# The recurrent group of a hybrid decoder layer, with the order of four engines written out by hand

## The chip, the cores and the metric

The kernel runs on one core of one Trainium2 chip. The metric is the device time of one execution in microseconds (us). Before the change it is 588.33 us, the median of three runs (588.04 to 588.38).

## The reference

One decoder layer for 512 tokens of width 1024, all in float32. The part that matters here, shortened:

```python
h = rms_norm(x, g_pre_mix)
q, k, v, xr, gr = split(h @ w_in)                # 512 columns each
attn = moba_attention(q, k, v, rel_bias)         # 8 heads of 64; causal, T5 bias
xr  = causal_dwconv(xr, w_conv_lru) + b_conv_lru # 4 taps along the tokens, per channel
r = sigmoid(blockdiag(xr, w_r) + b_r)            # 8 blocks of 64 channels
i = sigmoid(blockdiag(xr, w_i) + b_i)
log_a = -8 * r * softplus(-lam)
a, u = exp(log_a), sqrt(-expm1(2 * log_a)) * (i * xr)
lru = scan(h_t = a_t * h_(t-1) + u_t) * gelu(gr)
x = x + rms_norm(concat(attn, lru) @ w_out, g_post_mix)
x = x + rms_norm(ffn(rms_norm(x, g_pre_ffn)), g_post_ffn)   # 2816 hidden, conv of 3 taps, GLU
```

## The kernel before, in words

Tokens lie in four tiles of 128 (`NT`), the width in eight (`KD`). Each float32 product is three matmuls of a faster format: an operand is split into an upper part h (a cast on ACT, line 84) and a lower part l (a subtraction on DVE, line 85), and `mm3` (lines 79 to 81) adds hh, hl and lh in one PSUM bank. Weights are split in the same way (`split_w`), after a load of 1 MB on SP's queue into one of two `raw` buffers; the split parts have four buffers, `wh` and `wl`.

The recurrent group runs from the start to line 382. `norm_transpose` squares a token tile on ACT with a row sum, makes the reciprocal root in a few 128x1 steps on ACT and DVE (`rstd_of`), multiplies on DVE (`hn`), transposes on PE against the identity (`ptr`) and splits the result into `hT`. `keep_warm` puts matmuls on ones in between; the weight row `g_pre_mix` is spread over the partitions by four small matmuls (`gpre`, line 207). Small parameters come in rows and are transposed into `par`. `pfb` is the bias of each distance, `fb`, which goes to DRAM as `fbd` and is written out 128 times as `toep` for the attention.

For each of the four channel tiles the x branch is projected (`px`), convolved (line 325 on ACT, 327 three times on DVE), split (`xs`) and multiplied with the two gate matrices (`pg`, in the two "sc" banks); lines 337 to 348 turn that into decay and input, with the scales `kpos` and `kneg`. These come from a softplus of `lam`, a chain of 128x4 instructions on DVE (lines 270 to 287: a series in Horner form). The value projection (`pv`) and the gate branch (`pgr`, then GeLU) are 96 matmuls each. At the end the scan (line 381) and the product go to `mixT`. The attention follows: `head_pair` loads, splits and projects q and k (`pq`).

Nothing in this part has an order written by hand, but for the warm-ups and `gpre` (`keep_in_program_order`). The framework's scheduler lays out each engine's instructions by its own costs. PSUM has eight banks: three "mm", two "sc", two "tr", one "av"; whoever takes a bank waits for the readers of its last contents.

Of the kernel before, what the change touches and what calls it, by code (L numbers as in the profile page):

```python
# [12 lines left out]
F32 = mybir.dt.float32  # L13
# [5 lines left out]
P = 128  # L19
# [33 lines left out]
def hybrid_layer(  # L53
# [51 lines left out]
    nc.sync.dma_start(g_row, g_pre_mix)  # L105
    nc.sync.dma_start(xres[:, 0], x_v[:, 0])
# [27 lines left out]

    def norm_transpose(t, g, hT, pool):

        hn = pool.tile([P, D], F32, tag="hn", name="hn", bufs=4)
        sq = pool.tile([P, D], BF16, tag="sqn", name="sqn")
        ss = cp.tile([P, 1], F32, tag="ss", name="ss", bufs=8)
        nc.scalar.activation(sq, xres[:, t], AF.Square, accum_out=ss)  # L140
        r = rstd_of(ss, consts, "rpre")
        w = D // len(g)
        for n, gn in enumerate(g):
            hs = slice(n * w, (n + 1) * w)
            nc.vector.scalar_tensor_tensor(
                hn[:, hs], xres[:, t, hs], r, gn, op0=ALU.mult, op1=ALU.mult)
# [34 lines left out]
    nc.gpsimd.memset(graw, 0.0)  # L181
    for g, w in enumerate((w_r[0], w_i[0])):
        wv = w.rearrange("(t b) c d -> b c t d", b=2)
        for b in range(2):
            nc.sync.dma_start(graw[64 * b:64 * b + 64, g, :, 64 * b:64 * b + 64], wv[b])
# [6 lines left out]
    warm = pp.tile([P, 512], BF16, name="warm")
    nc.vector.memset(warm, 1.0)
    pwarm = bank("pwarm", "av")

    def keep_warm(n):

        for _ in range(n):
            tc.keep_in_program_order(nc.tensor.matmul(
                pwarm, warm[:, 0:P], warm, start=True, stop=True))  # L200

    keep_warm(3)
    ones = cp.tile([1, P], F32, name="ones")
    nc.vector.memset(ones, 1.0)
    gpre = [bank(f"gpre{n}", "sc") for n in range(2)]
    for n in range(2):
        tc.keep_in_program_order(nc.tensor.matmul(
            gpre[n], ones, g_row[:, n * 512:(n + 1) * 512], start=True, stop=True))
    keep_warm(4)

    for t in range(NT):
        norm_transpose(t, gpre, hT, pp)
        if t < 2:
            keep_warm(3)

    split(gw[0], gw[1], graw)
# [16 lines left out]
    nc.vector.tensor_copy(par, ppar[:, 0:80 + P])  # L233

# [72 lines left out]
    gl = lp.tile([P, NT, S], F32, name="gl")  # L307

    def xr_block(t):
        return split_w(raw_xr[t // 2][:, :, (t % 2) * P:(t % 2 + 1) * P], KD, P), bank("px", "mm")  # L310

    first = [xr_block(t) for t in range(2)]
    for c0, c1 in ((0, S // 2), (S // 2, S)):
        for w, px in first:
            project(w, px, c0, c1)
    for t in range(NT):
        if t < 2:
            px = first[t][1]
        else:
            if t == 2:  # L320
                raw_xr.append(load_raw(w_in[:, XR0 + 256:XR0 + 512], KD, 256))
            w, px = xr_block(t)
            project(w, px)
        c = xc[:, t]
        nc.scalar.activation(c, px, AF.Identity, scale=w_conv_l(3, t), bias=col(16 + t))
        for d in range(1, 4):
            nc.vector.scalar_tensor_tensor(
                c[:, d:], px[:, :S - d], w_conv_l(3 - d, t), c[:, d:], op0=ALU.mult, op1=ALU.add)
        xs = [lp.tile([P, S], F32R, tag=f"xs{i}", name=f"xs{i}") for i in "hl"]
        split(xs[0], xs[1], c)  # L330
        pg = [bank(f"pg{g}", "sc") for g in range(2)]
        for g in range(2):
            mm3(pg[g], at(gw, slice(None), g, t), (xs[0], xs[1]), True, True)


        a, g, y = av[:, t], gv[:, t], gl[:, t]
        nc.vector.tensor_scalar(a, pg[0], col(20 + t), 0.0, op0=ALU.add, op1=ALU.min)
        nc.scalar.activation(g, pg[0], AF.Abs, scale=0.5, bias=half_b[:, t:t + 1])
        nc.scalar.activation(y, pg[1], AF.Tanh, scale=0.5, bias=half_b[:, 4 + t:5 + t])
        nc.vector.scalar_tensor_tensor(c, y, 1.0, c, op0=ALU.add, op1=ALU.mult)  # L340
# [4 lines left out]
        nc.scalar.activation(a, g, AF.Exp, scale=kneg(t))  # L345
        nc.scalar.activation(g, g, AF.Tanh, scale=kpos(t))
# [4 lines left out]
    pv = [bank(f"pv{t}", ("tr", "tr", "av", "mm")[t]) for t in range(NT)]  # L351
    for c in range(2):
        raw = load_raw(w_in[c * 512:(c + 1) * 512, 2 * DA:3 * DA], 4, DA)
        for u in range(2):
            w = split_w(raw[:, 2 * u:2 * u + 2], 2, DA)
            for j in range(2):
                k = 4 * c + 2 * u + j
                for t in range(NT):
                    mm3(pv[t], at(hT, slice(None), k, slice(t * P, (t + 1) * P)),
                        at(w, slice(None), j), k == 0, k == KD - 1)  # L360

    def gr_block(t):
        if t % 2 == 0:
            raw_gr.append(load_raw(w_in[:, GR0 + t * P:GR0 + t * P + 256], KD, 256))
        return split_w(raw_gr[-1][:, :, (t % 2) * P:(t % 2 + 1) * P], KD, P)

    raw_gr = []
    w_gr = [gr_block(t) for t in range(NT)]
    for t in range(NT):
        src = pv[t].rearrange("p (a s d) -> p a s d", s=2, d=DH)  # L370
# [336 lines left out]
```

## Time and profile before

| | before |
|---|---|
| median of three runs | 588.33 us |
| profiled execution | 589.05 us, span 587.3 us |
| PE (TensorE matmul) | 574.3 us busy, 98% of the span |
| DVE / ACT / POOL | 360.1 (61%) / 278.4 (47%) / 2.8 us (0%) |
| DMA moved | 59.62 MB, mean 102 GB/s |

The span is the time that the profile covers. PE's busy time counts pipelined matmuls with a modelled end, so the distance between starts tells its pace better than the busy share. L84 is line 84 of the kernel. `hTh` and `hTl` are the two parts of `hT`. In brackets stands the idle time ahead of an instruction, and what ended it.

### The profile page before, as it was taken

What the parts mean: (1) busy time and instruction counts of PE and PEld (TensorE: products, weight loads), DVE (VectorE), ACT (ScalarE), POOL (GpSimd) and SP (SyncE); (2) the same over time, 40 slices, a digit from 0 to 9 for tenths busy, and PEclk for the clock granted to TensorE, in tenths of its full rate; (3) what the DMA queues carried; (4) which work ended last, traced back from release to release, by engine and by line L of the source; (5) the groups of instructions that cost most, each with busy time, mean ns of one, the idle gap of its engine ahead of it and who ended that gap; (6) DMA issues with size and microseconds to landing.
All of it is one profiled execution on the core that took longest, in us unless ns stands there. A gap on an engine that the chain in (4) does not pass through costs nothing.

```text
span 587.3 us, 7000 instructions
## 1 busy us (share of the span) xinstructions
PE 574.3 (98%) x2717; PEld 472.0 (80%) x2717; DVE 360.1 (61%) x665; ACT 278.4 (47%) x455; POOL 2.8 (0%) x10
## 2 busy tenths in 40 slices
PE   8999999999999999999999999999999999999995
PEld 4877888777788879988888888888888888888884
DVE  5969694798896895656656656656656521241225
ACT  6639953777775762534434443443444322132121
POOL 1000000000000000000000000000000000000000
PEclk9999999999999999999999999999999999999999
DMA  7562436233100624003413413412424223232103
GB/s 235 195 212 72 144 99 186 73 108 108 56 17 25 211 89 144 1 15 129 143 30 114 145 40 104 143 50 95 144 68 137 82 72 105 94 125 71 37 0 143
DMA packets 52265, 59.62 MB, mean 102 GB/s; under 512 B 2448, under 2 KB 41568, under 8 KB 52233
## 3 DMA queue, kind: packets, MB, share of 16 engines
q1 hardware_dynamic: 51201, 57.61, 30.3%
q10 hardware_dynamic: 1032, 1.57, 0.8%
q8 instruction: 21, 0.34, 0.2%
q14 instruction: 11, 0.09, 0.0%
HBM read 57.06 MB, written 3.69 MB: 103 GB/s over the span
## 4 chain that ended last, share of the span: by engine, by line
PE 90%; DVE 4%; ACT 3%; DMA 2%; issue 1%; DVEq 0%
PE pup L80 14%; PE pup L81 14%; PE pup L79 14%; PE py L80 8%; PE py L81 8%; PE py L79 8%; PE pq L79 2%; PE pq L80 2%; PE pq L81 2%; PE pav L471 2%; DMA raw<-in_w_up_dram 2%; PE ptp L461 1%; PE px L81 1%; PE px L79 1%; PE px L80 1%; PE pv L79 1%
## 5 line engine op out<-in xcount | busy, mean ns | idle before, releaser
L85 DVE TENSOR_TENSOR wl<-raw,wh 128x1024 fp32r<-128x1024 f32 x82 | 100.1, 1221 | 124.8 <-ACT wh L84 124.5
L84 ACT CAST wh<-raw 128x1024 fp32r<-128x1024 f32 x82 | 85.6, 1048 | 143.3 <-PE py L81 72.2
L81 PE MATMUL pup<-h2Th,wl 128*128 128x512 f32 x320 | 124.5, 389 | 0.0
L80 PE MATMUL pup<-h2Tl,wh 128*128 128x512 f32 x320 | 124.5, 389 | 0.0
L79 PE MATMUL pup<-h2Th,wh 128*128 128x512 f32 x320 | 124.3, 389 | 0.0
L80 PEld LDWEIGHTS pup<-h2Tl,wh 128*128 128x128 f32 x320 | 60.1, 188 | 12.5
L79 PEld LDWEIGHTS pup<-h2Th,wh 128*128 128x128 f32 x320 | 60.0, 188 | 12.5
L81 PEld LDWEIGHTS pup<-h2Th,wl 128*128 128x128 f32 x320 | 60.1, 188 | 12.3
L79 PE MATMUL py<-wh,acth 128*128 128x512 f32 x176 | 68.9, 391 | 0.0
L81 PE MATMUL py<-wh,actl 128*128 128x512 f32 x176 | 68.8, 391 | 0.0
L80 PE MATMUL py<-wl,acth 128*128 128x512 f32 x176 | 68.8, 391 | 0.0
L79 PEld LDWEIGHTS py<-wh,acth 128*128 128x128 f32 x176 | 33.1, 188 | 7.2
L81 PEld LDWEIGHTS py<-wh,actl 128*128 128x128 f32 x176 | 33.1, 188 | 7.2
L80 PEld LDWEIGHTS py<-wl,acth 128*128 128x128 f32 x176 | 33.1, 188 | 7.2
L629 DVE SCALAR_TENSOR_TENSOR yu<-pup,par,yu 128x511 f32<-128x511 f32 (+1 forms) x44 | 33.0, 749 | 4.3 <-ACT yu L627 3.5
L636 ACT ACTIVATE yg<-yg 128x512 f32<-128x512 f32 x22 | 13.9, 633 | 45.0 <-DVE yg L629 45.0
L629 DVE SCALAR_TENSOR_TENSOR yg<-pup,par,yg 128x511 f32<-128x511 f32 (+1 forms) x44 | 32.8, 746 | 2.0 <-ACT yg L627 1.2
L637 DVE TENSOR_TENSOR yu<-yu,yg 128x512 f32<-128x512 f32 x22 | 15.2, 692 | 18.3 <-ACT yg L636 18.3
L79 PE MATMUL pq<-hTh,wh 128*128 128x512 f32 x64 | 25.4, 397 | 0.0
L81 PE MATMUL py<-wh,mixTl 128*128 128x512 f32 x64 | 25.4, 396 | 0.0
L81 PE MATMUL pq<-hTh,wl 128*128 128x512 f32 x64 | 25.3, 395 | 0.0
L79 PE MATMUL py<-wh,mixTh 128*128 128x512 f32 x64 | 25.2, 394 | 0.0
(199 smaller groups left out, 940.2 us busy)
## 6 DMA issues: line engine op xcount, KB each, us to landing
raw<-in_w_up_dram SPq DMA_DIRECT2D x22, 1024.0 KB, 5.2
raw<-in_w_down_dram SPq DMA_DIRECT2D x10, 1024.0 KB, 5.3
raw<-in_w_in_dram SPq DMA_DIRECT2D x5, 1024.0 KB
rawqk<-in_w_in_dram SPq DMA_DIRECT2D x8, 512.0 KB, 5.3
raw<-in_w_out_dram SPq DMA_DIRECT2D x4, 1024.0 KB, 4.9
xres<-in_x_dram SPq DMA_DIRECT2D x4, 512.0 KB, 5.4
out_dram<-yz SPq DMA_DIRECT2D x8, 256.0 KB, 2.0
toep<-fbd ACTq DMA_DIRECT2D x1, 1536.0 KB
```

The costliest lines, as they stand in the source:

```text
L79: nc.tensor.matmul(o, lh, rh, start=start, stop=False)
L80: nc.tensor.matmul(o, lh, rl, start=False, stop=False)
L81: nc.tensor.matmul(o, ll, rh, start=False, stop=stop)
L84: nc.scalar.copy(h, src)
L85: (sub or nc.vector).tensor_sub(l, src, f32(h))
L461: nc.tensor.transpose(ptr[:, j * P:(j + 1) * P], st[:, j * P:(j + 1) * P], ident)
L471: nc.tensor.matmul(pav[:, j * P:], vs, pT[i][:, j * S:j * (S - P) + S], start=j == 0 and i == 0, stop=j == NT - 1 and i == 1)
L629: nc.vector.scalar_tensor_tensor(y[:, d:], pt[:, :S - d], w_conv_f(2 - d, blk), y[:, d:], op0=ALU.mult, op1=ALU.add)
L636: nc.scalar.activation(yg, yg, AF.Gelu_apprx_tanh)
L637: nc.vector.tensor_mul(yu, yu, yg)
```

## The change

From the first load to `mixT` the kernel now stands in `tc.manual_schedule` for PE, ACT, DVE and SP: each of these issues its instructions of this part in the order in which the program names them. POOL's order, and where instructions from outside the part fall between them, stay with the scheduler. To write such an order the loops are taken apart into small functions, called in the order wanted:

- `g_row` is loaded on ACT's queue; token tile 0 comes in two halves and is squared in two halves. The x branch's weights are four loads of 512 KB, one for each channel tile, ahead of the parameter rows and the gate matrices.
- The x products of channel tiles 0 to 2 run in token halves C0 (tiles 0 and 1) and C1; within one, products go by kind (hh, hl, lh) and not by `k`. Channel tile 3 keeps 512 columns.
- Two subtractions go from DVE to POOL: the lower part of channel tile 0's weights and that of the gate matrices. So does the softplus chain, but for the reciprocal.
- Gates of a channel tile stand between the quarters of the value projection. `toep` is issued on SP behind the last weights. Each tile's scan and product follow its own GeLU.

The core of the diff ("..." marks what is left out; the functions `norm`, `turn`, `upper`, `lower`, `conv_first`, `conv_rest`, `xs_upper`, `xs_lower`, `gates`, `sigmoids` and `decay` hold the old instructions unchanged; several calls stand in one line here):

```diff
-    nc.sync.dma_start(g_row, g_pre_mix)
-    nc.sync.dma_start(xres[:, 0], x_v[:, 0])
+    written.enter_context(tc.manual_schedule(engines={EN.PE, EN.Activation, EN.DVE, EN.SP}))
+    nc.scalar.dma_start(g_row, g_pre_mix)
+    for n in range(2):
+        hs = slice(n * 512, (n + 1) * 512)
+        nc.sync.dma_start(xres[:, 0, hs], x_v[:, 0, hs])
     nc.sync.dma_start(xres[:, 1], x_v[:, 1])
...
+    load_xr(0)
+    load_xr(1)
     nc.sync.dma_start(xres[:, 2], x_v[:, 2])
+    load_xr(2)
     nc.sync.dma_start(xres[:, 3], x_v[:, 3])
+    load_xr(3)
...
+    keep_warm(3)
+    gpre = [bank(f"gpre{n}", "sc") for n in range(2)]
+    for n in range(2):
+        nc.tensor.matmul(gpre[n], ones, g_row[:, n * 512:(n + 1) * 512], start=True, stop=True)
+    keep_warm(3)
...
+    def xr_lower(t, eng):
+        eng.tensor_sub(w_x[t][1], xr_cols(t), f32(w_x[t][0]))
...
+    def px_products(t, c0, c1, todo, first, last):
+        cs = slice(c0, c1)
+        for n, (k, i) in enumerate(todo):
+            nc.tensor.matmul(p_x[t][:, cs], w_x[t][i == LH][:, k], hT[i == HL][:, k, cs],
+                             start=first and n == 0, stop=last and n == len(todo) - 1)
...
+    sums(0, 2); rstd(0, 2); sums(1, 1); norm(0, 0); rstd(1, 1)
+    turn(0, 0, "tr"); keep_warm(3); norm(1, 0); norm(0, 1); upper(0, 0); lower(0, 0)
+    xr_upper(0); xr_lower(0, nc.gpsimd); turn(1, 0, "tr"); upper(1, 0); turn(0, 1, "mm")
+    upper(0, 1); norm(1, 1); lower(1, 0); lower(0, 1)
+    px_products(0, *C0, [(k, HH) for k in range(4)], True, False)
+    turn(1, 1, "av"); upper(1, 1); lower(1, 1)
+    px_products(0, *C0, [(k, HL) for k in range(4)] + [(k, HH) for k in range(4, 8)]
+                + [(k, LH) for k in range(4)] + [(k, HL) for k in range(4, 8)]
+                + [(k, LH) for k in range(4, 8)], False, True)
+    xr_upper(1); xr_lower(1, nc.vector); px_products(1, *C0, BY_KIND, True, True)
+    sums(2, 1); rstd(2, 1); norm(2, 0); norm(2, 1); xr_upper(2); xr_lower(2, nc.vector)
+    turn(2, 0, "tr"); turn(2, 1, "tr"); upper(2, 0); upper(2, 1); lower(2, 0); lower(2, 1)
+    px_products(2, *C0, BY_KIND, True, True)
+    sums(3, 1); rstd(3, 1); norm(3, 0); norm(3, 1); turn(3, 0, "tr"); turn(3, 1, "tr")
+    upper(3, 0); upper(3, 1); lower(3, 0); lower(3, 1)
+    px_products(0, *C1, BY_KIND, True, True)
     ppar = bank("ppar", "av")
...
+    px_products(1, *C1, BY_KIND, True, True)
+    px_products(2, *C1, BY_KIND, True, True)
+    xr_upper(3); xr_lower(3, nc.vector)
...
+    conv_first(0); conv_rest(0)
+    nc.scalar.copy(gw[0], graw)
+    nc.gpsimd.tensor_sub(gw[1], graw, f32(gw[0]))
+    nc.scalar.activation(sp[:, 2], sp[:, 1], AF.Exp, scale=-1.0)
+    conv_first(1); xs_upper(0); conv_rest(1); xs_lower(0)
+    nc.scalar.mul(fb[:, 0:S], pfb[0:H, :], 1.0 / ISCALE)
+    v_split(0); conv_first(2); conv_rest(2)
+    nc.gpsimd.tensor_scalar(sp[:, 3], sp[:, 2], 2.0, None, op0=ALU.add)
+    nc.vector.reciprocal(sp[:, 4], sp[:, 3])
+    nc.gpsimd.tensor_mul(sp[:, 3], sp[:, 2], sp[:, 4])
+    nc.gpsimd.tensor_mul(sp[:, 4], sp[:, 3], sp[:, 3])
+    nc.gpsimd.tensor_scalar(sp[:, 5], sp[:, 4], 2.0 / (2 * NS + 1), None, op0=ALU.mult)
+    for n in range(NS - 1, 0, -1):
+        nc.gpsimd.tensor_scalar(sp[:, 5], sp[:, 5], 2.0 / (2 * n + 1), None, op0=ALU.add)
+        nc.gpsimd.tensor_mul(sp[:, 5], sp[:, 5], sp[:, 4])
...
+    nc.gpsimd.tensor_scalar(sp[:, 6], sp[:, 5], LRU_C / 2, None, op0=ALU.mult)
+    nc.gpsimd.tensor_scalar(sp[:, 7], sp[:, 5], -LRU_C / 2, None, op0=ALU.mult)
+    p_x[3] = bank("px", "mm")
+    px3(0); gates(0); px3(1); v_split(1); xs_upper(1); xs_lower(1); sigmoids(0); gates(1)
+    conv_first(3); conv_rest(3); decay(0); xs_upper(2); xs_lower(2); v_products(0)
+    v_split(2); sigmoids(1); gates(2); xs_upper(3); xs_lower(3); v_products(1)
+    v_split(3); decay(1); gates(3); sigmoids(2); gr_split(0); v_products(2)
+    decay(2); sigmoids(3); gr_split(1); v_products(3); decay(3)
+    nc.scalar.activation(gv, gv, AF.Sqrt, scale=0.25)
...
+    nc.sync.dma_start(fbd, fb)
+    nc.sync.dma_start(toep, fbd[:, None, FE - EW:FE].to_broadcast([H, P, EW]))
...
+    written.close()
```

## Rows read from the trace of the kernel before

**Rows 1.** The page's chain that ended last: share of the span by engine.
```profile
PE 90%; DVE 4%; ACT 3%; DMA 2%; issue 1%; DVEq 0%
```
**Rows 2.** Windows: length, busy time (x instructions) per engine, PEclk, DMA share, GB/s.
```profile
0.00:15.00 15.00, 12.47 (x36) 6.03 (x36) 8.35 (x23) 10.32 (x20) 1.74 (x8) 1.00 0.77 230
...
40.00:42.00 2.00, 0.69 (x3) 0.30 (x2) 0.34 (x1) 1.56 (x2) 0.00 (x0) 1.00 0.49 186
42.00:92.00 50.00, 50.00 (x220) 40.82 (x219) 40.83 (x53) 36.39 (x54) 0.00 (x0) 1.00 0.37 107
```
**Rows 3.** Timeline of PE: start us, us, engine, line, operation, out<-in, shapes.
```profile
23.00 1.02 PE L254 MATMUL pfb<-oh,rb 32*8 32x512 f32 x2
23.95 0.39 PE L79 MATMUL px<-hTh,wh 128*128 128x256 f32 x1
...
29.80 0.40 PE L79 MATMUL px<-hTh,wh 128*128 128x512 f32 x1
...
69.94 0.39 PE L79 MATMUL pgr<-hTh,wh 128*128 128x512 f32 x1
...
91.70 0.39 PE L79 MATMUL pq<-hTh,wh 128*128 128x512 f32 x1
```
**Rows 4.** Timeline of PE, the first 15 us.
```profile
2.92 3.78 PE L207 MATMUL gpre<-g_row,ones 1*128 1x512 f32 x4
6.63 1.89 PE L199 MATMUL pwarm<-warm 128*128 128x512 bf16 x4
...
8.30 1.91 PE L151 MATMUL ptr<-ident,hn 128*128 128x128 f32 x8
10.01 1.49 PE L199 MATMUL pwarm<-warm 128*128 128x512 bf16 x3
...
13.25 0.60 PE L151 MATMUL ptr<-ident,hn 128*128 128x128 f32 x4
...
14.95 0.39 PE L81 MATMUL px<-hTh,wl 128*128 128x256 f32 x1 [0.33 <-DVE wl L85]
```
**Rows 5.** Timelines of ACT and of DVE: the first square and the first product.
```profile
4.59 1.06 ACT L140 ACTIVATE sqn<-xres 128x1024 bf16<-128x1024 f32 x1 [2.35 <-DMA xres<-in_x_dram]
...
6.81 1.41 DVE L145 SCALAR_TENSOR_TENSOR hn<-xres,rpre,gpre 128x512 f32<-128x512 f32 x2
```
**Rows 6.** Timeline of PE, the longest wait behind the first products.
```profile
41.72 0.70 PE L79 MATMUL pg<-xsh,gwh 128*128 128x512 f32 x2 [1.31 <-issue]
```
**Rows 7.** Groups of POOL: line, operation, shapes, count | busy us, mean ns | idle.
```profile
L401 POOL MEMSET klz<- 64x512 f32 x2 | 1.0, 521 | 94.0 <-DVE mixTl L85 93.9
L181 POOL MEMSET graw<- 128x1024 f32 x1 | 1.0, 955 | 0.0
masks.py:199 POOL TENSOR_SCALAR_AFFINE_SELECT ident<-ident 128x128 f32<-128x128 f32 x1 | 0.3, 293 | 0.0
...
L256 POOL MEMSET fb<- 8x128 f32 x1 | 0.2, 194 | 0.0
L694 POOL MEMSET const-bfloat16-1.0<- 128x1 bf16 x1 | 0.1, 112 | 0.0
```
**Rows 8.** Groups of DVE from 24 to 62 us, shapes kept apart.
```profile
L85 DVE TENSOR_TENSOR wl<-raw,wh 128x1024 fp32r<-128x1024 f32 x8 | 9.8, 1220 | 0.0
...
L327 DVE SCALAR_TENSOR_TENSOR xc<-px,par,xc 128x511 f32<-128x511 f32 x4 | 2.9, 745 | 0.7 <-ACT xc L325 0.6
...
L340 DVE SCALAR_TENSOR_TENSOR xc<-gl,xc 128x512 f32<-128x512 f32 x3 | 2.1, 688 | 0.4 <-ACT gl L339 0.4
...
L281 DVE SCALAR_TENSOR_TENSOR sp<-sp 128x4 f32<-128x4 f32 x8 | 1.3, 161 | 0.2
```
**Rows 9.** Groups of ACT up to 76 us, shapes kept apart.
```profile
L84 ACT CAST wh<-raw 128x1024 fp32r<-128x1024 f32 x12 | 12.4, 1045 | 3.4 <-DMA raw<-in_w_in_dram 2.9 <-PE pv L81 0.5
L84 ACT CAST hTh<-ptr 128x512 fp32r<-128x512 f32 x8 | 4.7, 584 | 6.2 <-PE ptr L151 6.1
...
L345 ACT ACTIVATE av<-gv,sp 128x512 f32<-128x512 f32 x4 | 2.9, 724 | 0.0
```

More of the change, by code (lines that the diff above doesn't have):

```diff
@@ L180, in hybrid_layer @@
     graw = gp.tile([P, 2, NT, P], F32, name="graw")
[L181 to L185, printed above, removed]
     gw = [gp.tile([P, 2, NT, P], F32R, name=f"gw{i}") for i in "hl"]
+    fb = gp.tile([H, FE], F32, name="fb")
     pre_stack = attn_stack.enter_context(ExitStack())
     pp = pre_stack.enter_context(tc.tile_pool(name="pp", bufs=1))
[L192 to L216, printed above, removed]
     rows = pp.tile([P, 2, P], F32, name="rows")
@@ L228, in hybrid_layer @@
     nc.sync.dma_start(rows[:, 1], wcf[0:P])
-    par = cp.tile([P, 80 + P], F32, name="par")
+    nc.gpsimd.memset(graw, 0.0)
+    for g, w in enumerate((w_r[0], w_i[0])):
+        wv = w.rearrange("(t b) c d -> b c t d", b=2)
+        for b in range(2):
+            nc.sync.dma_start(graw[64 * b:64 * b + 64, g, :, 64 * b:64 * b + 64], wv[b])
+    par = cp.tile([P, 80 + P], F32, name="par")
+    rb = pp.tile([NB, H], F32, name="rb")
+    oh = pp.tile([NB, S], F32, name="oh")
+    nc.sync.dma_start(rb, rel_bias)
@@ new lines, in hybrid_layer, with keep_warm @@
+    nc.sync.dma_start(oh, onehot)
+    warm = pp.tile([P, 512], BF16, name="warm")
+    nc.vector.memset(warm, 1.0)
+    pwarm = bank("pwarm", "av")
+    def keep_warm(n):
+        for _ in range(n):
+            nc.tensor.matmul(pwarm, warm[:, 0:P], warm, start=True, stop=True)
+    ones = cp.tile([1, P], F32, name="ones")
+    nc.vector.memset(ones, 1.0)
+    keep_warm(3)
+    gpre = [bank(f"gpre{n}", "sc") for n in range(2)]
+    for n in range(2):
+        nc.tensor.matmul(gpre[n], ones, g_row[:, n * 512:(n + 1) * 512], start=True, stop=True)
@@ new lines, in hybrid_layer, with sums, rstd @@
+    keep_warm(3)
+    hn, ssn, rn, pt = {}, {}, {}, {}
+    def sums(t, parts):
+        hn[t] = pp.tile([P, D], F32, tag="hn", name="hn", bufs=4)
+        ssn[t] = cp.tile([P, 4], F32, tag="ss", name="ss", bufs=8)
+        square(t, ssn[t], parts, pp)
+    def rstd(t, parts):
+        ss = ssn[t]
+        if parts == 2:
+            for i, f in ((2, 1.0), (3, -0.5)):
+                nc.vector.tensor_scalar(
+                    ss[:, i:i + 1], ss[:, 0:1], f / D, f * EPS, op0=ALU.mult, op1=ALU.add)
+            rn[t] = rstd_of(ss[:, 1:2], ss[:, 2:4], "rpre")
+        else:
+            rn[t] = rstd_of(ss[:, 0:1], consts, "rpre")
@@ new lines, in norm, with turn, upper, lower @@
+    def norm(t, half):
+        normalised(hn[t], t, rn[t], gpre[half], slice(512 * half, 512 * half + 512))
+    def turn(t, half, tag):
+        pt[t, half] = bank("ptr", tag)
+        transposes(hn[t], half, pt[t, half])
+    def upper(t, half):
+        nc.scalar.copy(hT[0][part(t, half)], by_rows(pt[t, half]))
+    def lower(t, half):
+        sl = part(t, half)
+        nc.vector.tensor_sub(hT[1][sl], by_rows(pt[t, half]), f32(hT[0][sl]))
+    w_x, p_x = [None] * NT, [None] * NT
+    def xr_upper(t):
+        w_x[t] = [wp.tile([P, KD, P], F32R, tag=f"w{i}", name=f"w{i}") for i in "hl"]
+        nc.scalar.copy(w_x[t][0], xr_cols(t))
@@ new lines, in hybrid_layer @@
+    sums(0, 2)
+    rstd(0, 2)
+    sums(1, 1)
+    norm(0, 0)
+    rstd(1, 1)
+    turn(0, 0, "tr")
+    keep_warm(3)
+    norm(1, 0)
+    norm(0, 1)
+    upper(0, 0)
+    lower(0, 0)
+    xr_upper(0)
+    xr_lower(0, nc.gpsimd)
+    turn(1, 0, "tr")
+    upper(1, 0)
+    turn(0, 1, "mm")
+    upper(0, 1)
+    norm(1, 1)
+    lower(1, 0)
+    lower(0, 1)
+    p_x[0] = bank("px", "mm")
+    px_products(0, *C0, [(k, HH) for k in range(4)], True, False)
+    turn(1, 1, "av")
+    upper(1, 1)
+    lower(1, 1)
@@ L230, in hybrid_layer @@
+    upper(2, 0)
+    upper(2, 1)
+    lower(2, 0)
+    lower(2, 1)
+    p_x[2] = bank("px", "mm")
+    px_products(2, *C0, BY_KIND, True, True)
+    sums(3, 1)
+    rstd(3, 1)
+    norm(3, 0)
+    norm(3, 1)
+    turn(3, 0, "tr")
+    turn(3, 1, "tr")
+    upper(3, 0)
+    upper(3, 1)
+    lower(3, 0)
+    lower(3, 1)
+    px_products(0, *C1, BY_KIND, True, True)
     ppar = bank("ppar", "av")
@@ L307, in hybrid_layer @@
     gl = lp.tile([P, NT, S], F32, name="gl")
[L309 to L325, printed above, removed]
+    xs, p_g = [None] * NT, [None] * NT
@@ L326, in hybrid_layer, with conv_first, conv_rest @@
+    def conv_first(t):
+        nc.scalar.activation(xc[:, t], p_x[t], AF.Identity, scale=w_conv_l(3, t), bias=col(16 + t))
+    def conv_rest(t):
         for d in range(1, 4):
             nc.vector.scalar_tensor_tensor(
[L328 to L331, printed above, removed]
+                xc[:, t, d:], p_x[t][:, :S - d], w_conv_l(3 - d, t), xc[:, t, d:],
+                op0=ALU.mult, op1=ALU.add)
@@ L332, in hybrid_layer, with xs_upper, xs_lower, gates @@
+    def xs_upper(t):
+        xs[t] = [lp.tile([P, S], F32R, tag=f"xs{i}", name=f"xs{i}") for i in "hl"]
+        nc.scalar.copy(xs[t][0], xc[:, t])
+    def xs_lower(t):
+        nc.vector.tensor_sub(xs[t][1], xc[:, t], f32(xs[t][0]))
+    def gates(t):
+        p_g[t] = [bank(f"pg{g}", "sc") for g in range(2)]
         for g in range(2):
-            mm3(pg[g], at(gw, slice(None), g, t), (xs[0], xs[1]), True, True)
+            mm3(p_g[t][g], at(gw, slice(None), g, t), xs[t], True, True)
+    def sigmoids(t):
@@ L343, in hybrid_layer, with decay @@
         nc.vector.scalar_tensor_tensor(g, g, 1.0, a, op0=ALU.add, op1=ALU.mult)
[L345 to L346 removed]
+    def decay(t):
+        a, g, y = av[:, t], gv[:, t], gl[:, t]
+        nc.scalar.activation(a, g, AF.Exp, scale=sp[:, 7, t:t + 1])
+        nc.scalar.activation(g, g, AF.Tanh, scale=sp[:, 6, t:t + 1])
         nc.scalar.activation(y, a, AF.Square)
         nc.vector.scalar_tensor_tensor(g, y, 1.0, g, op0=ALU.add, op1=ALU.mult)
[L351 removed]
@@ L352, in hybrid_layer @@
[L352 to L362, printed above, removed]
+    raw_v = [load_raw(w_in[c * 512:(c + 1) * 512, 2 * DA:3 * DA], 4, DA) for c in range(2)]
@@ new lines, in hybrid_layer, with v_split, v_products @@
+    w_v, p_v = [None] * 4, []
+    def v_split(u):
+        w_v[u] = split_w(raw_v[u // 2][:, 2 * (u % 2):2 * (u % 2) + 2], 2, DA)
+    def v_products(u):
+        if u == 0:
+            p_v.extend(bank(f"pv{t}", ("tr", "tr", "av", "mm")[t]) for t in range(NT))
+        for j in range(2):
+            k = 2 * u + j
+            for t in range(NT):
+                mm3(p_v[t], at(hT, slice(None), k, slice(t * P, (t + 1) * P)),
+                    at(w_v[u], slice(None), j), k == 0, k == KD - 1)
@@ new lines, in hybrid_layer @@
+    conv_first(0)
+    conv_rest(0)
+    nc.scalar.copy(gw[0], graw)
+    nc.gpsimd.tensor_sub(gw[1], graw, f32(gw[0]))
+    nc.scalar.activation(sp[:, 2], sp[:, 1], AF.Exp, scale=-1.0)
+    conv_first(1)
+    xs_upper(0)
+    conv_rest(1)
+    xs_lower(0)
+    nc.scalar.mul(fb[:, 0:S], pfb[0:H, :], 1.0 / ISCALE)
+    v_split(0)
+    conv_first(2)
+    conv_rest(2)
+    nc.gpsimd.tensor_scalar(sp[:, 3], sp[:, 2], 2.0, None, op0=ALU.add)
+    nc.vector.reciprocal(sp[:, 4], sp[:, 3])
+    nc.gpsimd.tensor_mul(sp[:, 3], sp[:, 2], sp[:, 4])
@@ new lines, in hybrid_layer @@
+    nc.gpsimd.tensor_add(sp[:, 5], sp[:, 5], sp[:, 0])
+    nc.gpsimd.tensor_scalar(sp[:, 6], sp[:, 5], LRU_C / 2, None, op0=ALU.mult)
+    nc.gpsimd.tensor_scalar(sp[:, 7], sp[:, 5], -LRU_C / 2, None, op0=ALU.mult)
+    p_x[3] = bank("px", "mm")
+    px3(0)
+    gates(0)
+    px3(1)
+    v_split(1)
+    xs_upper(1)
+    xs_lower(1)
+    sigmoids(0)
+    gates(1)
+    conv_first(3)
+    conv_rest(3)
+    decay(0)
+    xs_upper(2)
+    xs_lower(2)
+    v_products(0)
+    v_split(2)
+    sigmoids(1)
@@ new lines, in hybrid_layer @@
+    gates(2)
+    xs_upper(3)
+    xs_lower(3)
+    v_products(1)
+    v_split(3)
+    decay(1)
+    gates(3)
+    sigmoids(2)
+    gr_split(0)
+    v_products(2)
+    decay(2)
+    sigmoids(3)
+    gr_split(1)
+    v_products(3)
+    decay(3)
+    nc.scalar.activation(gv, gv, AF.Sqrt, scale=0.25)
+    for t in range(NT):
+        nc.vector.tensor_mul(xc[:, t], xc[:, t], gv[:, t])
+        if t == 1:
+            gr_split(2)
+    fbd = dp.tile([H, FE], F32, name="fbd")
+    nc.sync.dma_start(fbd, fb)
@@ L371, in hybrid_layer @@
+    toep = dp.tile([H, P, EW], F32, name="toep")
+    nc.sync.dma_start(toep, fbd[:, None, FE - EW:FE].to_broadcast([H, P, EW]))
+    for t in range(NT):
+        src = p_v[t].rearrange("p (a s d) -> p a s d", s=2, d=DH)
         h, l = vhl[:, t, :, 0:4:3, :], vhl[:, t, :, 1:3, :]
```

128 lines of the change are left out of this document (65 added, 63 removed).

## The prediction

> **What bounds the kernel now.** I read the share of busy time first, then the chain, then TensorE's own order in the stretch that the change rewrites. TensorE (PE) is the engine to watch: 90% of the chain that ended last is its work [rows 1]. The windows show where it is not full: 2.5 of the first 15 us without a matmul, 1.3 of the 2 us from 40 to 42, and nothing from 42 to 92 [rows 2]. The clock's mean is 1.00 in each of them, so a matmul's price is read from distances between starts: 0.12 us for 256 columns (48 products from 23.95 to 29.80) and 0.227 for 512 (96 gate-branch products from 69.94 to 91.70) [rows 3]. Early on it is twice that: three warm-up matmuls take 1.28 us from 10.01 (0.427 each), eight transposes 1.71 us from 8.30 (0.21 each), where four take 0.44 us from 13.25 (0.11 each). That is the lower of the clock's two levels, 1.2 GHz, up to about 13 us, and 2.4 GHz after it [rows 4].
>
> The recurrent group ends on PE at 91.70, where the first q product follows without a gap [rows 3], and what comes after is PE's too. So I take each microsecond by which that point moves as a microsecond of the kernel. The profiled execution took 589.05 us around a span of 587.3, and the median is 588.33; the sum is a difference within the span and is put on the median.
>
> **The start.** g_row leaves SP for ACT's queue, so token tile 0 is issued 0.4 us sooner, in two halves, and is squared in two halves. Before, the square began at 4.59 and the first normalised half was begun at 6.81 [rows 5]. I take the second half's square (about 0.63 us, a little over half of 1.06) to begin at 4.4; with the accumulator's 0.19 and the same 1.04 us from root to product, hn is begun near 6.3 and its half is done by 7.0. That does not decide, because PE isn't ready: g_row's four matmuls run until 6.63 [rows 4] and three warm-ups stand behind them in the written order. PE's own list then sets the pace: 6.63 + 3 x 0.427 = 7.92; four transposes at 0.22 to 8.80; three warm-ups to 10.08; eight transposes to 11.84; four products at 0.235 to 12.78; the last four transposes, in which the clock rises, to 13.44. The casts that these need (0.58 each) and xr's 1.05 us cast come between 8.9 and 12.5 and keep up. xr's lower part goes to POOL: its price lies between 0.95 (POOL's memset of that shape would be the floor) and 2.3 us (the 128-column POOL row of 0.293, eight times); begun at 10.5 it is wanted at about 14.3, so it is hidden up to 3.8. I cost it at nothing.
>
> Before, the dense stretch began at 14.95 with two xr products done [rows 4]; now it begins at 13.44 with four. What both still have to do differs only in xr: 94 halves and 48 wholes before (11.28 + 10.88 = 22.16 us), 140 halves and 24 wholes now (16.80 + 5.44 = 22.24). The rest is the same work: 24 gate, 96 value and 96 gate-branch products (216 x 0.227 = 48.96), 16 transposes (1.76), the parameters' two transposes (0.5) and the bias product (0.95 to the next start [rows 3]): 52.2 us. Before: 14.95 + 22.16 + 52.2 = 89.3, so 91.70 holds 2.4 us of stalls, 1.31 of them one visible wait at the first gate product [rows 6]. Now: 13.44 + 22.24 + 52.2 = 87.9, plus whatever the written order makes PE wait.
>
> **The waits of the written order**, laid out instruction by instruction with the prices of [rows 8, 9], less 0.08 us where one follows at once on the same engine.
> (a) Token tile 1's second cast comes 0.40 us after PE wants it.
> (b) Token tile 3: ACT may square it only behind tile 2's casts, which wait for tile 2's transposes. Tile 2 is turned from 19.0; casts to 20.8; square, accumulator and root to 22.4; DVE's three small steps and the norm to 23.5. PE has finished the third xr tile's first half at 22.7. It waits 0.9, then 0.2 and 0.4 between the halves: 1.5.
> (c) gates(1) writes the two "sc" banks that gates(0) filled, which are read by sigmoids(0), on DVE behind conv_rest(2), v_split(1) and xs_lower(1). DVE: parameters copied at 28.5, xr 3's lower part, three conv taps for tile 0 (to 32.2) and tile 1 (32.8 to 34.8), v_split(0) to 37.8, taps for tile 2 to 39.8, the reciprocal to 39.9, v_split(1) to 41.1, xs_lower(1) to 41.7, sigmoids' first step to 42.4. PE is there at 41.74 and goes on at 42.50: 0.8.
> These make 2.65 us, about what there was before.
>
> (d) **The softplus chain.** 17 small DVE instructions, of the kind of the Horner steps' 0.16 us [rows 8], become 26 on POOL, the eight steps and the closing one two each; the reciprocal stays on DVE, behind the taps of tile 2. So 25 POOL instructions, each needing the last, start at 39.9 only. Their result is the scale of decay(0), the next work on ACT after conv_first(3), which ends at 44.4; behind it on ACT's list stand xs_upper(2) and v_split(2), and behind those on DVE sg_a(1), which frees the bank for gates(2). The trace of before has no small arithmetic on POOL. From below: 0.11 us, the memset of one column. From above: 0.52, klz's memset of 512 columns. The nearest row is the affine select, the only POOL instruction there that reads and writes SBUF: 0.293 [rows 7]. I take that: 25 x 0.293 = 7.3, so ACT gets its scale at 47.3 and not at 44.4. Then decay(0) to 49.4, xs_upper(2) and v_split(2)'s cast to 50.9, its lower part on DVE to 52.2, sg_a(1) to 52.9, gates(2) at 53.0. PE has ended v_products(0) at 42.50 + 1.36 + 5.44 = 49.3: it waits 3.7 us. Were the chain free, ACT's and DVE's other work would still make it wait 0.74. At 0.11 us an instruction this is the case, at 0.52 the wait is 9.4.
>
> (e) The gate branch: scans move between the products; DVE and ACT have 5.44 us for each tile's 3 to 4 us of work. toep's transfer moves from ACT's queue at 27 us to SP behind the last weights, at about 60; it is wanted near 96. Nothing, unless the attention's first splits suffer (a rival).
>
> **Sum.** 87.9 + 2.65 + 3.7 = 94.2, against 91.70: 2.5 us later. 588.33 + 2.5 = 590.8.
>
> **Rivals.**
> 1. POOL's chain is short enough (not slower). It decides at 0.19 us an instruction: below that gates(2) waits under 1.2 us and the early start pays. Without any wait for POOL PE ends at 87.9 + 2.65 + 0.74 = 91.25, so 587.9; if the 1.5 us at tile 3 close too (a tile 2 cast sooner is enough), 586.4. For it: the small memset's 0.11 and DVE's 0.16; against it: every POOL row that handles more than a column is at 0.19 or above.
> 2. POOL's chain is held up by DVE. From 39.9 on DVE runs four instructions that read two SBUF operands (v_split(1) 1.15, xs_lower(1), sg_c(0) and sg_g(0) 0.62 each): 3.0 us. If POOL stands still in them, PE's wait is 6.7 and the time 593.8. No row of before shows the two engines at work together. The Trainium skill's page "SBUF — State Buffer", section "Who interferes with whom", states this rule: a DVE instruction with two SBUF inputs and a GpSimd instruction that reads SBUF share one port, and whichever comes second is blocked for the whole of the first; no run here shows it yet.
> 3. What follows is pushed back: the attention's first weights are split only behind the written part's last instructions on ACT and DVE, which end some 3 us after PE's last product (gelu, product, cast, subtraction). With 1.05 + 1.22 for the first split PE stands 5.3 us: with rival 1's order, 593.2. Against it: the order is fixed among the written instructions only, and their data are ready 10 us earlier.
>
> **Chances.** The forecast's mechanism (0.2 to 0.42 us an instruction) 50%, its own range 588.5 to 594; rival 1 30%, rival 2 or a still dearer chain 14%, rival 3 6%. A measurement tells this kernel from no change at about 0.2%, 1.2 us. Faster by that: most of rival 1 with another stall closed, 0.20. Within: the rest of it and the cheap end of the forecast, 0.20. Slower: 0.60. The range, 586.6 to 595.6, leaves out the dearest chains and the best of rival 1.
>
> **What would show it.** POOL's group on sp: 25 and one instructions with a start every 0.29 us, and ACT's first exponent of decay(0) released by POOL. One gap of 3 to 4 us on PE, before the third pair of gate products, and gaps under 1 us at tile 3 and gates(1). The first dense xr products near 13.4. The forecast is wrong if PE's last gate-branch product comes before 91.5, or if the gap stands and the released engine is DVE with POOL long done; and if both move as written while the span does not, the attention gave it back.

## The result, and the profile after

The changed kernel takes 614.51 us (median of 4 runs, 613.58 to 615.17) where the kernel before takes 588.36 beside it: a ratio of 1.0442, 95% interval 1.0424 to 1.046. 590.8 was predicted, with 586.6 to 595.6 as its range: the direction was right, the size wrong by 24 us. First three lines of the page of the changed kernel: TensorE's busy time, the clock by slices, the chain by engine.

```profile
PE 580.5 (95%) x2737; PEld 477.0 (78%) x2737; DVE 358.7 (59%) x648; ACT 279.7 (46%) x457; POOL 15.0 (2%) x38
...
PEclk9989899599999999999999999999999999999998
...
PE 85%; DVE 5%; ACT 5%; DMA 2%; issue 1%; POOL 1%; DVEq 0%; SPq 0%; ACTq 0%
```

PE's share of the chain fell from 90% [rows 1] to 85%, and up to the last slice the granted clock is lowest in slices 3, 5 and 8 of 40 (15.3 us each; the eighth near half). Timeline of PE, changed kernel:

```profile
11.55 0.74 PE L306 MATMUL px<-hTh,wh 128*128 128x256 f32 x4 [0.24 <-ACT hTh L284]
...
12.52 0.74 PE L306 MATMUL px<-hTl,wh 128*128 128x256 f32 x4
13.41 0.74 PE L306 MATMUL px<-hTh,wh 128*128 128x256 f32 x4
...
22.97 1.28 PE L156 MATMUL ptr<-ident,hn 128*128 128x128 f32 x8 [0.75 <-DVE hn L150]
...
33.44 1.02 PE L391 MATMUL pfb<-oh,rb 32*8 32x512 f32 x2
...
37.77 0.74 PE L79 MATMUL px<-hTh,wh 128*128 128x512 f32 x1 [3.31 <-ACT sp L483]
...
47.94 0.50 PE L79 MATMUL pg<-xsh,gwh 128*128 128x512 f32 x1 [1.51 <-ACT gv L437]
...
60.01 0.79 PE L79 MATMUL pg<-xsh,gwh 128*128 128x512 f32 x1 [4.95 <-ACT gv L437]
...
103.12 0.39 PE L81 MATMUL pgr<-hTh,wl 128*128 128x512 f32 x1
...
113.84 0.79 PE L79 MATMUL pq<-hTh,wh 128*128 128x512 f32 x1 [10.34 <-ACT wh L84]
114.43 0.63 PE L80 MATMUL pq<-hTl,wh 128*128 128x512 f32 x1
```

By 13.41 eight x products are done. The first q product begins at 113.84; before, it began at 91.70 [rows 3]. Five waits stand between (the brackets: length, and what ended it), 20.9 us together. After three of them the clock is at its lower level. Windows of the changed kernel (length, busy time of PE, PEld, DVE, ACT and POOL, then PEclk, DMA share and GB/s):

```profile
37.50:41.50 4.00, 3.73 (x9) 2.97 (x10) 3.13 (x6) 3.99 (x8) 1.35 (x2) 0.57 0.00 0
60.00:64.00 4.00, 3.99 (x9) 3.14 (x10) 1.76 (x3) 2.60 (x5) 0.00 (x0) 0.50 0.00 0
...
114.00:119.00 5.00, 4.96 (x11) 3.46 (x12) 2.27 (x2) 1.39 (x2) 0.00 (x0) 0.50 1.12 302
120.00:124.00 4.00, 4.00 (x20) 3.29 (x19) 2.87 (x3) 2.49 (x3) 0.00 (x0) 1.00 0.79 204
```

PE counts as busy throughout, yet it starts 11 products in 5 us from 114 and 20 in 4 us from 120. PEclk 0.50 is 1.2 of 2.4 GHz: a product of 512 columns every 0.43 us and not 0.227. "Busy" hides this; the clock's column shows it.

**Who made PE wait.** Timeline of ACT:

```profile
34.50 0.78 ACT L412 ACTIVATE xc<-px,par 128x512 f32<-128x512 f32 x1 [8.68 <-PE pfb L391]
...
53.86 0.72 ACT L447 ACTIVATE av<-gv,sp 128x512 f32<-128x512 f32 x1 [3.69 <-POOL sp L507]
...
104.96 0.62 ACT L84 CAST mixTh<-gl 128x512 fp32r<-128x512 f32 x1 [0.76 <-DVE gl L564]
112.75 1.04 ACT L84 CAST wh<-rawqk 128x1024 fp32r<-128x1024 f32 x1 [7.17 <-DMA rawqk<-in_w_in_dram]
```

Timeline of SP's queue, and under it one row of its waits (engine, line, waited for: total, times, longest):

```profile
70.94 0.76 SPq L551 DMA_DIRECT2D toep<-fbd  x1
106.38 0.36 SPq L589 DMA_DIRECT2D tb<-fbd  x1
106.84 0.42 SPq L597 DMA_DIRECT2D rawqk<-in_w_in_dram  x1
```

```profile
SPq L589 <- DVE mixTl L85: 34.6, 1, 34.6
```

- The first convolution tap (34.50) needs the parameters and the xr product, both long there; its releaser is the bias product pfb, which it reads nothing of. As the program reads, the tap's output xc is put into memory that the preparation's pool gave up just ahead of it, and the last reader in that pool is pfb (rb and oh). No view shows addresses; e2 tests it. The written order puts pfb behind all halves of xr, at 33.44; before, it ran at 23.00 [rows 3].
- decay(0) (53.86) waits for POOL's chain, as predicted, and gates(2) behind it.
- The first q weights (112.75) wait for their own transfer, though the DMA engines stand idle from 82 to 106 us (share 0.00): its issue at 106.84 stands on SP behind that of tb, the attention's bias tile, which waits 34.6 us for the recurrent group's memory, until its last reader, DVE's last subtraction. The written order ends with that group, and nothing in it asks for the q weights. Before, they were asked for ahead of tb; why the scheduler, which orders what lies outside the written part, now puts tb first is not shown. Timeline of SP's queue, kernel before:

```profile
62.39 32.66 SPq L414 DMA_DIRECT2D rawqk<-in_w_in_dram  x8
96.09 0.37 SPq L406 DMA_DIRECT2D tb<-fbd  x1
```

POOL's chain and the DVE instructions beside its first two steps (two timelines):

```profile
44.88 1.08 POOL L495 TENSOR_TENSOR sp<-sp 128x4 f32<-128x4 f32 x1 [6.03 <-DVE sp L494]
46.04 0.52 POOL L496 TENSOR_TENSOR sp<-sp 128x4 f32<-128x4 f32 x1
46.65 0.23 POOL L498 TENSOR_SCALAR sp<-sp 128x4 f32<-128x4 f32 x1
46.96 0.23 POOL L500 TENSOR_SCALAR sp<-sp 128x4 f32<-128x4 f32 x1
...
53.61 0.22 POOL L507 TENSOR_SCALAR sp<-sp 128x4 f32<-128x4 f32 x1
```

```profile
44.71 1.19 DVE L85 TENSOR_TENSOR wl<-raw,wh 128x1024 fp32r<-128x1024 f32 x1
45.82 0.68 DVE L425 TENSOR_TENSOR xsl<-xc,xsh 128x512 fp32r<-128x512 f32 x1
```

Undisturbed, a step starts every 0.28 to 0.31 us. Four of 24 (from 44.88, 46.04, 48.73 and 49.64) take 0.52 to 1.08 instead of 0.20 to 0.23: each lies under one DVE instruction with two SBUF operands and ends 0.06 to 0.08 us behind it. That is 2.0 us of the chain's 8.95.

### The profile page after: what moved, and what is told of

Its sections match the earlier page's. It is cut to its first block, busy times and chain, and to the rows that moved or that the text cites. A ratio compares the mean times of both kernels' runs of the same rounds, so it can differ in the third digit from the quotient of the medians.

```text
span 612.3 us, 7064 instructions
## 1 busy us (share of the span) xinstructions
PE 580.5 (95%) x2737; PEld 477.0 (78%) x2737; DVE 358.7 (59%) x648; ACT 279.7 (46%) x457; POOL 15.0 (2%) x38
## 4 chain that ended last, share of the span: by engine, by line
PE 85%; DVE 5%; ACT 5%; DMA 2%; issue 1%; POOL 1%; DVEq 0%; SPq 0%; ACTq 0%
PE pup L80 13%; PE pup L81 13%; PE pup L79 13%; PE py L81 8%; PE py L79 8%; PE py L80 8%; PE px L306 2%; PE pq L79 2%; PE pq L80 2%; PE pq L81 2%; PE pav L654 2%; PE ptp L644 1%; PE pgr L81 1%; PE pgr L80 1%; PE pgr L79 1%
## 5 line engine op out<-in xcount | busy, mean ns | idle before, releaser
L85 DVE TENSOR_TENSOR wl<-raw,wh 128x1024 fp32r<-128x1024 f32 x78 | 95.3, 1221 | 125.1 <-ACT wh L84 124.8
L84 ACT CAST wh<-raw 128x1024 fp32r<-128x1024 f32 x78 | 81.6, 1047 | 140.2 <-PE py L81 72.2
L80 PE MATMUL pq<-hTl,wh 128*128 128x512 f32 x64 | 26.0, 407 | 0.0
L820 DVE TENSOR_TENSOR yu<-yu,yg 128x512 f32<-128x512 f32 x22 | 15.3, 693 | 18.0 <-ACT yg L819 18.0
```

What stands on the lines that cost most here:

```text
L80: nc.tensor.matmul(o, lh, rl, start=False, stop=False)
L84: nc.scalar.copy(h, src)
L85: (sub or nc.vector).tensor_sub(l, src, f32(h))
L820: nc.vector.tensor_mul(yu, yu, yg)
```

## The experiments

Times are medians; ratios are to the kernel before in the same session (588.3 to 588.9 us). A gain over the changed kernel compares two sessions and is known to about 1 us.

### The q weights' loads first: e1_qk_first

```diff
     def head_pair(pr):
+        raw = ...; nc.sync.dma_start(raw[:, :, i], ...)   # i in 0, 1
         tb = ap_.tile(...)
         nc.sync.dma_start(tb ...)
-        raw = ...; nc.sync.dma_start(raw[:, :, i], ...)
```

> The changed kernel, and the attention's loads of q and k weights named ahead of the loads of its bias tile tb. Theory: on SP the first tb load, which waits for memory of the recurrent group (released by its last mixT subtraction at 105.6 us), stands ahead of the first q/k load, so TensorE idles 10.5 us before the first q product and then runs 13 products at half rate (some 2.7 us). Then q products follow the gate branch without a gap, and 614.5 falls by 13 to 601 (600 to 603). Rival: the q/k loads are late because their buffers come free late, or because of what stands ahead on ACT; then the order of naming is worth under 3 us (above 611).

609.60 us, ratio 1.0346 (1.0325 to 1.0368): 4.9 gained and not 13, between the theory and its rival. The loads go out at 79.6, but PE still waits 3.07 us for ACT's split, which is placed behind the written part's last cast, and later 1.90 for pair 1. The loads were only a part of this loss.

### The bias product ahead of the parameters: e2_bias_product_early

```diff
+    pfb = bank("pfb", "tr")
+    nc.tensor.matmul(pfb[0:H, :], rb, oh, start=True, stop=True)
     ppar = bank("ppar", "av")
```

> The changed kernel, and the bias product pfb (with a tr bank) named ahead of the parameters' transposes ppar, not behind the last half of the x products. Theory: the first convolution writes into memory that the preparation's pool gave up, whose last reader is pfb; so it waited until 34.5 us for a product that has nothing to do with it. Now it starts near 29.4; the 3.3 us gap on TensorE before the fourth x tile and the half-rate products behind it go (3 us), and the gates come 5 us sooner, until the softplus chain on POOL holds decay(0) as the prediction had it: 614.5 falls by 6 to 9 (605.5 to 608.5). Rival: the convolution waited for a product queued ahead of pfb on TensorE, or for the parameters: then it starts within 1 us of 34.5 and the time stays above 613.

609.36 us, 1.0342 (1.0320 to 1.0365), just above the expected range. The first tap begins at 29.80, released by the parameters' copy, though that copy comes 1.6 us later than in the changed kernel: it was pfb that held the tap. Timeline of ACT in e2:

```profile
29.80 0.78 ACT L412 ACTIVATE xc<-px,par 128x512 f32<-128x512 f32 x1 [3.48 <-DVE par L372]
```

The wait of 3.31 us is gone, those of 4.94 and 10.27 stay. The memory that the first tap waited for cost 5.2 us: its wait, and the slow products behind it (9 products in 3.74 us from 37.77, 1.7 us more than at 0.227).

### The chain begun earlier: e3_reciprocal_early

```diff
     xs_upper(0)
+    nc.gpsimd.tensor_scalar(sp[:, 3], sp[:, 2], 2.0, None, op0=ALU.add)
+    nc.vector.reciprocal(sp[:, 4], sp[:, 3])
     conv_rest(1)
```

> The changed kernel, and the one DVE instruction of the softplus chain, the reciprocal, named ahead of the convolution of channel tile 1 and not behind that of tile 2. Theory: POOL is quick enough (0.30 us a start), it only began too late; the chain now runs from about 39 to 47 us, decay(0) isn't held (it was until 53.9), the gap before gates(2) falls from 5 to about 1 us and the half-rate stretch behind it goes: 614.5 falls by 4 to 6 (608.5 to 610.5). Rival: POOL blocked by DVE is what costs; then the chain stretches by another 3 us or more and the gain is under 2 us (above 612.5).

609.56 us, 1.0343 (1.0320 to 1.0365), as expected: 5.0 us for the late start of the softplus chain. The chain is no shorter (from 39.59 to 49.23), but done before decay(0) wants it. The wait of 4.95 us goes; that at gates(1) grows to 1.93, with slow products behind it, and one of 0.20 at gates(3) comes.

### The three together: e4_all_three

> The three edits together. Theory: they are the whole of the loss; TensorE ends the gate branch near 91.5 us, the q products follow, and the time is that of the kernel before within 2 us (586.5 to 590.5). Rival: the written order loses elsewhere too (waits at token tile 3 and at the gates, the second pair's weights behind tb on SP): 591 to 597.

600.16 us, 1.0188 (1.0166 to 1.0210): the rival's kind of loss, and more than its range held. Timelines of PE and of ACT:

```profile
97.04 0.78 PE L79 MATMUL pq<-hTh,wh 128*128 128x512 f32 x1 [3.07 <-ACT wh L84]
...
114.39 0.80 PE L627 MATMUL psc<-sk,sq 128*128 128x128 f32 x2 [2.28 <-ACT sk L617]
```

```profile
95.42 0.62 ACT L84 CAST mixTh<-gl 128x512 fp32r<-128x512 f32 x1 [0.76 <-DVE gl L564]
95.95 1.99 ACT L84 CAST wh<-rawqk 128x1024 fp32r<-128x1024 f32 x2
104.19 1.05 ACT L84 CAST wh<-rawqk 128x1024 fp32r<-128x1024 f32 x1 [6.25 <-DMA rawqk<-in_w_in_dram]
```

The casts of pair 0 begin as the written part's last cast ends, though their data were asked for at 70.0; those of pair 1 hold ACT for 6.25 us, their loads standing behind tb again.

### The weights inside the written part: e5_qk_in_group, e8_qk_in_group_alone

```diff
             gr_split(2)
+    raw_qk[0] = load_qk(0)
...
     gr_split(3)
+    raw_qk[1] = load_qk(1)
     for t in range(NT):
...
         split(mixT[0][:, 4 + t], mixT[1][:, 4 + t], gl[:, t])
+        w_qk[t // 2].append(split_w(raw_qk[t // 2][:, :, t % 2], KD, P))
```

e5 has this and the edits of e2 and e3; e8 is the changed kernel with this alone.

> All three of the earlier edits (600.16 us), and now the loads of the q and k weights of head pairs 0 and 1 stand in the written order: pair 0's behind the last gate-branch load, pair 1's behind the last gate-branch split, both ahead of every bias load; and the four splits stand one behind each of the gate branch's four token tiles. Theory: TensorE's wait of 3.07 us ahead of the q products and the one of 2.28 us ahead of the scores go, and with them the products at half rate (the q and k products took 78.9 us there, 75.8 in the kernel before): 600.2 - 3.1 - 2.3 - 3.1 = 591.7, range 590 to 593.5. Rival: ScalarE, which now waits with each split for a weight buffer that the gate branch's products free, comes late to the gelu and the mixer's splits, and the bias loads behind the written part's end make the scores wait: 595 to 600.

> The changed kernel with only the q and k weights of pairs 0 and 1 (loads and splits) brought into the written order; the other two edits are not made. Theory: the wait of 10.34 us ahead of the q products and the half rate behind it (79.0 us of q and k products against 75.8) go: 614.5 - 10.3 - 3.2 = 601.0, range 599 to 603. Rival: naming only the loads ahead gave 609.6; if the splits' place matters little, 606 to 610.

e5: 590.19 us, 1.004 (1.0026 to 1.0054). e8: 600.70 us, 1.0207 (1.0192 to 1.0223): 13.8 us for the weights' place. Both as the theory had it. Timelines of SP and PE in e5:

```profile
68.90 0.99 SPq L474 DMA_DIRECT2D rawqk<-in_w_in_dram  x2
...
79.97 10.59 SPq L474 DMA_DIRECT2D rawqk<-in_w_in_dram  x4
97.72 0.37 SPq L601 DMA_DIRECT2D tb<-fbd  x1
```

```profile
42.70 0.50 PE L79 MATMUL pg<-xsh,gwh 128*128 128x512 f32 x1 [1.81 <-ACT gv L437]
...
92.70 0.39 PE L79 MATMUL pq<-hTh,wh 128*128 128x512 f32 x1
```

The bias tables come last and PE does not wait for them; the q products follow at 92.70 without a gap, 1.0 us later than before [rows 3].

### The same instructions, order free: e6_free_order

```diff
-    written.enter_context(tc.manual_schedule(engines={EN.PE, EN.Activation, EN.DVE, EN.SP}))
```

> The changed kernel with the line that holds four engines to the written order taken out: the same instructions, buffers and POOL work, but the order is the planner's again. Theory (the loss lies in the fixed order: the bias load ahead of the weights on SP's queue, ScalarE and VectorE held to the written part's end): the wait of 10.3 us ahead of the q products goes and most of the waits for the gates too, 588 to 597. Rival (the loss lies in what was rewritten, the POOL chain and the memory that the first convolution tap waits for): 603 to 612, with the waits of 3.3 and 4.95 us still there.

593.21 us, 1.0081 (1.0066 to 1.0096). 21.3 of the 26.2 us lost come with the fixed order. The other 4.8, with the new instructions in the planner's order, were not taken apart. The planner asks for the q weights ahead of tb; its longest wait on PE is 3.17 us, for a gate-branch split.

### All of the wait filled, or most: e10_fill_the_wait, e11_fill_all_of_it

```diff
+    fill = bank("fill", "sc")
+    for _ in range(40):          # e11: 48
+        nc.tensor.matmul(fill, hT[0][:, 0, 0:P], hT[0][:, 1], start=True, stop=True)
     written.close()
```

> The changed kernel, with 40 products of 128x512 whose result nobody reads put behind the gate branch's last tile (9.1 us at 0.227 us each, inside the wait of 10.34 us). Theory (the q products behind the wait run at the clock's lower level because TensorE stood still, and would not if it hadn't): the q products' half rate goes, 614.5 - 3.2 = 611.3, range 610 to 612.5. Rival (the lower level there has another reason, such as the transfers and splits at that time): 614 to 615, and the q products stay 0.43 us apart.

> As the fill of 40 products, but with 48 (10.9 us, from 102.8 to 113.7 in that trace), so that no wait over 0.6 us is left ahead of the q products. With 40 the wait of 1.75 us that was left was still followed by 10 products of q 0.43 us apart. Theory (TensorE's standing still brings the lower level): all q products come 0.227 us apart, 612 us, range 611 to 613. Rival (the transfers and splits at that time bring it): products 0.43 us apart stay, 613.5 to 615.

e10: 614.04 us, 1.0432 (1.0412 to 1.0451), a miss: 1.75 us of waiting were left, another 0.53 behind the second q product, and then q products 0.43 us apart. e11: 613.08 us, 1.0417 (1.04 to 1.0435), just over the upper end of what was expected. Groups of the q products in the changed kernel, then in e11 (count | busy us, mean ns | idle before), and a window of e11 (PE alone):

```profile
L79 PE MATMUL pq<-hTh,wh 128*128 128x512 f32 x64 | 26.6, 416 | 10.3 <-ACT wh L84 10.3
L81 PE MATMUL pq<-hTh,wl 128*128 128x512 f32 x64 | 26.4, 412 | 0.0
L80 PE MATMUL pq<-hTl,wh 128*128 128x512 f32 x64 | 26.0, 407 | 0.0
```

```profile
L79 PE MATMUL pq<-hTh,wh 128*128 128x512 f32 x64 | 25.5, 398 | 0.2 <-ACT wh L84 0.2
L81 PE MATMUL pq<-hTh,wl 128*128 128x512 f32 x64 | 25.4, 398 | 0.5 <-DVE wl L85 0.5
L80 PE MATMUL pq<-hTl,wh 128*128 128x512 f32 x64 | 25.0, 391 | 0.0
```

```profile
116.00:120.00 4.00, 3.91 (x17) 1.00 0.98 260
```

The same products take 79.0 us behind the wait and 75.9 when PE has been kept at work, at full clock though the transfers run at 260 GB/s. PE's standing still brings the lower level, not the traffic; behind the wait of 4.95 us, too, the clock is at 0.50 while the DMA engines move nothing (60.00 to 64.00 above). In time e11 gives back only 1.4 of these 3.1 us: its q weights landed later, PE's first q product coming 11.5 us behind the last gate-branch product and not 10.7, and 0.53 us of waiting for their lower halves shows, which the slow products had covered.

### Values between the gates, and the values copied early: e7_value_products_between, e9_values_copied_early

```diff
     gates(0)
     px3(1)
...
+    v_products(0)
     gates(1)
...
-    v_products(0)
     v_split(2)
     sigmoids(1)
+    v_products(1)
     gates(2)
```

e7 is e5 with this, and so on for the other quarters. e9 is e7 with three moves: the splits of the four value banks and gr_split(2) stand around decay(3) instead of behind the square root; in sigmoids, ACT's Abs stands ahead of DVE's reading of the same bank; sums(3) and rstd(3) stand ahead of tile 2's transposes.

> The kernel with the q and k weights in the written order, and each quarter of the value products named one step earlier, so that 24 products of values (5.4 us of TensorE) lie between any two tiles of gates; before, gates 0 and 1 had only 12 products between them. Theory: the waits for the gates (1.81, 1.44 and 0.23 us with the three earlier edits) go because the sigmoids end under the values: 3.5 us less than the kernel it is made from, 587 to 589.5, at or below the kernel before. Rival: the last tile's gates come 5 us later in the order, the state's scan and the gate branch's product with it wait at the end, and the scores behind them: no gain, 590 to 594.

> The kernel with the value products between the gates (590.5 us), with three further moves in the written order: the split of the four value banks ahead of the last decay, so that a bank is free when the gate branch's third tile wants it; ScalarE's reading of a gate's bank named ahead of VectorE's; token tile 3's squares and root ahead of tile 2's copies. Theory: the wait of 1.99 us ahead of the third tile goes with the 9 products at half rate behind it (1.8 us), the waits of 0.23 and 0.75 us go: 590.5 - 4.8 = 585.7, range 584.5 to 588, under the kernel before (588.5). Rival: the value splits (2.0 us on ScalarE, 2.5 on VectorE) push the decay, the square root and the first gelu back, and the fourth tile or the q weights wait in its place: 589 to 592.

e7: 590.53 us, 1.0029 (1.0019 to 1.0039), no faster than e5 and in the rival's range, but not by its mechanism: the wait at gates(1) went, the one of 0.23 stayed, and PE, now earlier, had to wait at the third gate-branch tile for ACT's GeLU to free a bank. Timeline of PE in e7:

```profile
81.33 0.50 PE L79 MATMUL pgr<-hTh,wh 128*128 128x512 f32 x1 [1.99 <-ACT gl L573]
```

e9: **584.84 us, 0.9934 (0.9922 to 0.9946)**: 0.7% faster than the kernel before. The three moves were not tried one by one. Its timeline of PE and one window:

```profile
87.35 0.39 PE L79 MATMUL pq<-hTh,wh 128*128 128x512 f32 x1
```

```profile
15.00:88.00 73.00, 72.76 (x385) 62.08 (x384) 54.34 (x81) 49.31 (x72) 11.37 (x27) 1.00 0.42 130
```

PE works 72.76 of the 73 us at full clock, and q begins 4.35 us earlier than before [rows 3]. The POOL chain is in it: begun early, it no longer keeps PE waiting.

## Why the prediction was wrong

Two steps failed: (e), which set the end of the written part at nothing (13.8 us, e8), and the first line of (c), which let the first tap wait for its inputs only (5.2 us, e2). Step (d), which made the forecast slower than before, held and is worth 5.0 (e3).

The sum put the first q product at 94.2; it came 19.6 us later. Of these, 13.7 are the waits of 3.31 and 10.34, which were in no term. The waits that were priced, 6.35 us, came to 7.2 (0.75, 1.51 and 4.95). The slow products behind the waits of 3.31 and 4.95 make some 4.2; about 1 is left open.

The three causes add up within what the runs can tell: alone, their removal gains 5.2 (e2), 5.0 (e3) and 13.8 us (e8), 24.0 together, and e5, which removes all, gains 24.3. By the ratios, which take out the sessions, it is 25.5 against 23.7. What is left over the kernel before, 1.7 us, stands beside e5's wait of 1.81 at gates(1); e7 removed that wait, and another took its place.

- **The start came 0.5 us early.** 13.44, worked out by PE's own list, was the end of the last transposes, with four x products done; in the trace eight are done at 13.41 (0.12 us each). That the two numbers agree is luck. Tile 3 made PE wait 0.75, not 1.5.
- **Step (c) failed in its first line.** I let the taps of tile 0 follow the parameters' copy at 28.5. Here a written instruction also waited for its output's memory: xc's was held by pfb, which the change moved from 23.00 to 33.44. Cost 5.2 us, and the reciprocal came at 44.63 and not at 39.9.
- **Step (d): mechanism right, place late, one cost short.** 24 instructions hang on the reciprocal, not 25. 0.293 an instruction was taken; the undisturbed steps start 0.28 to 0.31 us apart. The price fits by luck: it was the duration of another operation on a larger tile, and a step here takes 0.20 to 0.23. Rival 2's standing still came on top, with 2.0 us of its 3.0. The wait at gates(2) was 4.95 us against 3.7. By the rule "Who interferes with whom" of the Trainium skill's page "SBUF — State Buffer" a DVE instruction with two SBUF inputs and a GpSimd instruction that reads SBUF contend, and the one issued first blocks the other. The trace agrees for DVE first: 1.08 and 0.52 us beside DVE's 1.19 and 0.68, and 0.20 to 0.23 beside taps that read PSUM.
- **Step (e) failed, and it is over half of the loss.** It was costed at nothing; rival 3 named ACT's split behind the written part, but at 6%, because "their data are ready 10 us earlier". They were not even asked for: SP is one of the four engines in the written order, and tb's load, waiting for memory, stood ahead of the weights. e1 shows that with the loads alone brought forward PE still waits for the splits; e8 moves both.
- **The clock's fall behind a wait was not in the sum.** The prediction took half rate for the first products only. Behind the waits of 3.31, 4.95 and 10.34 us PE worked at 1.2 GHz for 3.5 to 5.7 us each; behind the last one that costs 3.1 us (e11). For the first 15 us the clock's column shows 1.00 [rows 2] although the distances [rows 4] are double; there only the distances tell the pace.

## What to carry to other kernels

When an order is fixed by hand over a stretch, price its ends first: list what the stretch behind needs (loads, splits), and where those stand now on each in-order queue, the DMA queue too; a load that waits for memory holds the loads behind it on its queue, as tb's did here. For each moved instruction look up who last read the memory that its successors write, not only who makes their data. A wait of several us on TensorE is to be priced with the slow products behind it (here behind every wait of 3 us and more, and behind some of 1.8).

## What the runs showed that was not expected

- Products at half rate behind a wait: after 1.81 (e5), 1.93 (e3), 1.99 (e7) and the longer ones. After 1.51 (47.94, changed kernel), 1.69 (e11), and also 1.81 at the same gates in e4, the products came 0.23 us apart. So the length of the wait alone does not settle it; what else does is not shown here.
- POOL's 128x1024 subtraction of two operands takes 2.39 us, DVE's 1.22 [rows 8]; the prediction's upper bound was 2.3.
- ACT and DVE reading the same PSUM bank went one after the other in the order named: at 47.20 ACT had waited 2.83 us behind DVE's av.
